# Two load queues instead of one: x from Sync, y from Scalar, in a kernel that streams 512 MB

## The chip, the cores and the metric

The kernel runs on one core of a Trainium2 chip (the experiments ran on two chips, each round with the kernel before beside it). The metric is the device time in microseconds (us), the median of several executions. All executions quoted here are of the undisturbed state ("fast"); those of one kernel agreed within 0.06% of each other. Engines: ACT is ScalarE, DVE is VectorE, POOL is GpSimd, PE is TensorE, SP is SyncE. "SPq" and "ACTq" are the sequencers of SP and ACT while they issue a DMA. Each engine takes its instructions in the order in which the build laid them out; how much that can cost is seen below, where ACT stands still for about 9 us in front of one small instruction. "Lnn" is line nn of the kernel's file. A load has "landed" when its completion is signalled to the engines that wait for it.

## The reference

```python
# x, y: 8192 x 8192 float32
x_norm = np.linalg.norm(x, axis=1, keepdims=True)
y_norm = np.linalg.norm(y, axis=1, keepdims=True)
return np.sum(x * y, axis=1) / (x_norm.squeeze() * y_norm.squeeze() + 1e-8)
```

One cosine similarity per row. Every input byte is read once: 2 x 256 MB. Per row there are three sums, xx, yy and xy, and at the end xy / sqrt(xx * yy).

## The kernel before

The rows are cut into 64 tiles of 128 rows. A tile is one load of x (128 x 8192 float32, 4 MB) and one of y. ACT squares and sums x and y, DVE multiplies x by y and sums. There are two buffers for x and two for y, so tile t+2 can be loaded when tile t is used up.

```python
    XCH = [(0, HALF), (HALF, n_cols)]                     # last x: two halves
    Q = n_cols // 8                                       # last y: 3 x 1 MB, 2 x 0.5 MB
    YCH = [(0, 2 * Q), (2 * Q, 4 * Q), (4 * Q, 6 * Q), (6 * Q, 7 * Q), (7 * Q, n_cols)]

    def issue_dma(t):
        if t == last:
            for a, b in XCH:
                nc.sync.dma_start(out=xtiles[t][:, a:b], in_=xv[t, :, a:b])
            for a, b in YCH:
                nc.sync.dma_start(out=ytiles[t][:, a:b], in_=yv[t, :, a:b])
        else:
            nc.sync.dma_start(out=xtiles[t], in_=xv[t])
            nc.sync.dma_start(out=ytiles[t], in_=yv[t])
    ...
    def compute_tile(t):            # DVE: sum(x*y); ACT: sum(x*x), then sum(y*y)
    ...
    def chain(cols, ps, sb, orows): # closes the tiles in cols
        nc.vector.tensor_tensor(out=nn[:, cols], in0=xx_acc[:, cols], in1=yy_acc[:, cols],
                                op=mybir.AluOpType.mult)
        nc.scalar.activation(out=den[:, cols], in_=nn[:, cols],
                             func=mybir.ActivationFunctionType.Sqrt)
        nc.vector.reciprocal(out=rcp[:, cols], in_=den[:, cols])
        ...                         # times xy on DVE, transpose on PE, copy, store
    for t in range(n_tiles - 1):
        if t + 2 < n_tiles:
            issue_dma(t + 2)
        compute_tile(t)
        if t == n_tiles - 3:        # early closing chain: tiles 0 to 61
            e = slice(0, last - 1)
            chain(e, res_t_ps[e, :], res_t[e, :], e)
    ...
    # last tile, in pieces. First: xx of columns 0:2048 on DVE, of 2048:4096 on ACT
    nc.scalar.activation(out=sq_s[:, HALF:], in_=xt[:, HALF:],        # second half of the last x
                         func=mybir.ActivationFunctionType.Square, accum_out=xxp[:, 2:3])
    for k, (a, b) in enumerate(YCH):
        nc.scalar.activation(out=sq_s[:, a:b], in_=yt[:, a:b], ...)       # yy of this piece
        nc.vector.tensor_tensor_reduce(... in0=xt[:, a:b], in1=yt[:, a:b] ...)  # xy of it
    ...                             # fold the pieces, close tiles 62 and 63, store
```

The early closing chain: one product `nn` on DVE, then one square root `den` on ACT, for the 62 tiles that are done. It is written after tile 61.

## Time and profile before

| | before |
|---|---|
| time, median | 1256.34 us |
| DMA engines busy | 99.5% |
| bytes per second over the span | 428 GB/s |
| ACT busy / DVE busy | 73% / 45% |
| period of a tile in the steady part | 19.4 us |

From the page of the kernel before: the span, the busy times, the bytes per second in 40 slices of the span, the one load queue, and the chain of waits that ended last.

```profile
span 1254.4 us, 933 instructions
...
PE 0.8 (0%) x2; PEld 0.2 (0%) x2; DVE 561.6 (45%) x147; ACT 915.0 (73%) x276; POOL 0.7 (0%) x6
...
GB/s 401 435 435 435 429 430 428 435 434 435 429 429 430 434 433 435 429 428 432 434 434 435 428 428 432 435 434 434 428 428 433 435 433 433 427 430 432 435 434 307
...
q1 hardware_dynamic: 19220, 536.91, 99.5%
...
DMA 76%; DVE 22%; SPq 1%; issue 1%; DVEq 0%; PE 0%; ACT 0%
```

The loads bind: the rate is level (427 to 435 GB/s) between the first slice and the last, and the chain is loads and the DVE product that frees the next buffer. Next, three groups of instructions of the same page (line, engine, operation, output and inputs, count; then busy us and mean ns of one; then idle us before them and what ended it).

```profile
L96 DVE CUSTOM_DVE_ANT_0 prod_s<-xt,yt 128x8192 bf16<-128x8192 f32 x63 | 547.6, 8692 | 687.5 <-DMA yt<-in_y_dram 687.5
L106 ACT ACTIVATE sq_s<-xt 128x8192 bf16<-128x8192 f32 x63 | 442.9, 7031 | 168.5 <-DMA xt<-in_x_dram 168.5
L112 ACT ACTIVATE sq_s<-yt 128x8192 bf16<-128x8192 f32 x63 | 443.0, 7031 | 164.2 <-DMA yt<-in_y_dram 164.2
```

ACT waits about 2.6 us twice a tile: x lands, is squared in 7.03 us, then y lands 9.7 us after x. What the end costs is read from the timeline of the kernel before (start us, length us, engine, line, operation; in brackets the idle time before it and what ended it):

```profile
1209.50 7.03 ACT L112 ACTIVATE sq_s<-yt 128x8192 bf16<-128x8192 f32 x1 [2.59 <-DMA yt<-in_y_dram]
1209.58 8.69 DVE L96 CUSTOM_DVE_ANT_0 prod_s<-xt,yt 128x8192 bf16<-128x8192 f32 x1 [10.72 <-DMA yt<-in_y_dram]
...
1218.20 0.22 DVE L120 TENSOR_TENSOR nn<-xx_acc,yy_acc 128x62 f32<-128x62 f32 x1
...
1218.45 0.26 ACT L124 ACTIVATE den<-nn 128x62 f32<-128x62 f32 x1 [1.83 <-DVE nn L120]
...
1219.22 7.03 ACT L106 ACTIVATE sq_s<-xt 128x8192 bf16<-128x8192 f32 x1 [0.51 <-DMA xt<-in_x_dram]
...
1228.94 7.03 ACT L112 ACTIVATE sq_s<-yt 128x8192 bf16<-128x8192 f32 x1 [2.60 <-DMA yt<-in_y_dram]
1228.99 8.69 DVE L96 CUSTOM_DVE_ANT_0 prod_s<-xt,yt 128x8192 bf16<-128x8192 f32 x1 [8.60 <-DMA yt<-in_y_dram]
...
1238.69 3.62 ACT L173 ACTIVATE sq_s<-xt 128x4096 bf16<-128x4096 f32 x1 [0.59 <-DMA xt<-in_x_dram]
...
1249.21 1.04 ACT L180 ACTIVATE sq_s<-yt 128x1024 bf16<-128x1024 f32 x1
```

The product and the square root of the early chain (L120, L124) run at 1218. When y of tile 62 lands at 1228.9, its x has long been squared. ACT's last square ends at 1250.25, about 2 us after the last bytes, and DVE's last product at 1250.77; the span ends 4.15 us after ACT's last square.

### The profile page before, as it was taken

What the parts mean: (1) busy time and instruction counts of PE and PEld (TensorE: products, weight loads), DVE (VectorE), ACT (ScalarE), POOL (GpSimd) and SP (SyncE); (2) the same over time, 40 slices, a digit from 0 to 9 for tenths busy, and PEclk for the clock granted to TensorE, in tenths of its full rate; (3) what the DMA queues carried; (4) which work ended last, traced back from release to release, by engine and by line L of the source; (5) the groups of instructions that cost most, each with busy time, mean ns of one, the idle gap of its engine ahead of it and who ended that gap; (6) DMA issues with size and microseconds to landing.
All of it is one profiled execution on the core that took longest, in us unless ns stands there. A gap on an engine that the chain in (4) does not pass through costs nothing.

```text
span 1254.4 us, 933 instructions
## 1 busy us (share of the span) xinstructions
PE 0.8 (0%) x2; PEld 0.2 (0%) x2; DVE 561.6 (45%) x147; ACT 915.0 (73%) x276; POOL 0.7 (0%) x6
## 2 busy tenths in 40 slices
PE   0000000000000000000000000000000000000000
PEld 0000000000000000000000000000000000000000
DVE  2354353443534535445354353453544525445356
ACT  5777767776777767776777767776777767776777
POOL 0000000000000000000000000000000000000000
DMA  9999999999999999999999999999999999999997
GB/s 401 435 435 435 429 430 428 435 434 435 429 429 430 434 433 435 429 428 432 434 434 435 428 428 432 435 434 434 428 428 433 435 433 433 427 430 432 435 434 307
DMA packets 19227, 536.97 MB, mean 428 GB/s; under 512 B 2132, under 2 KB 2196, under 8 KB 2452
## 3 DMA queue, kind: packets, MB, share of 16 engines
q1 hardware_dynamic: 19220, 536.91, 99.5%
q14 instruction: 7, 0.06, 0.0%
HBM read 536.87 MB, written 0.03 MB: 428 GB/s over the span
## 4 chain that ended last, share of the span: by engine, by line
DMA 76%; DVE 22%; SPq 1%; issue 1%; DVEq 0%; PE 0%; ACT 0%
DMA yt<-in_y_dram 76%; DVE prod_s L96 21%; SPq L63 1%; DVE prod_s L186 0%; DVEq L96 0%; SPq L64 0%; SPq L61 0%; SPq L59 0%; DVE xy_acc L96 0%; PE res_t_ps_last L221 0%; DVE res_row_last L222 0%; ACT den L212 0%; DVE rcp L216 0%; DVE res L217 0%; DVE xy_acc L204 0%
## 5 line engine op out<-in xcount | busy, mean ns | idle before, releaser
L96 DVE CUSTOM_DVE_ANT_0 prod_s<-xt,yt 128x8192 bf16<-128x8192 f32 x63 | 547.6, 8692 | 687.5 <-DMA yt<-in_y_dram 687.5
L106 ACT ACTIVATE sq_s<-xt 128x8192 bf16<-128x8192 f32 x63 | 442.9, 7031 | 168.5 <-DMA xt<-in_x_dram 168.5
L112 ACT ACTIVATE sq_s<-yt 128x8192 bf16<-128x8192 f32 x63 | 443.0, 7031 | 164.2 <-DMA yt<-in_y_dram 164.2
L112 ACT ACTIVATION_READ_ACCUMULATOR sq_s<-yt 128x1 f32 x63 | 11.8, 188 | 0.0
L106 ACT ACTIVATION_READ_ACCUMULATOR sq_s<-xt 128x1 f32 x63 | 11.8, 187 | 0.0
L186 DVE CUSTOM_DVE_ANT_0 prod_s<-xt,yt 128x2048 bf16<-128x2048 f32 (+1 forms) x5 | 9.2, 1864 | 1.6 <-DMA yt<-in_y_dram 1.5
L180 ACT ACTIVATE sq_s<-yt 128x2048 bf16<-128x2048 f32 (+1 forms) x5 | 7.8, 1551 | 0.0
L96 DVE DVE_READ_ACCUMULATOR2_ANT xy_acc<- 128x1 f32 x63 | 5.2, 83 | 0.0
L173 ACT ACTIVATE sq_s<-xt 128x4096 bf16<-128x4096 f32 x1 | 3.6, 3617 | 0.6 <-DMA xt<-in_x_dram 0.6
L157 DVE CUSTOM_DVE_ANT_0 prod_s<-xt 128x2048 bf16<-128x2048 f32 x1 | 2.3, 2291 | 0.0
L167 ACT ACTIVATE sq_s<-xt 128x2048 bf16<-128x2048 f32 x1 | 1.9, 1911 | 0.0
L70 ACT ACT_TABLE_LOAD x1 | 1.3, 1283 | 0.7 <-PEq L238 0.7
L124 ACT ACTIVATE den<-nn 128x62 f32<-128x62 f32 x1 | 0.3, 257 | 1.8 <-DVE nn L120 1.8
L71 ACT ACT_TABLE_LOAD x1 | 1.3, 1283 | 0.0
L133 PE MATMUL res_t_ps<-ident,res 128*62 128x128 f32 x1 | 0.4, 392 | 1219.7 <-DVE res L129 1219.7
L180 ACT ACTIVATION_READ_ACCUMULATOR sq_s<-yt 128x1 f32 x5 | 0.9, 186 | 0.0
L128 DVE RECIPROCAL rcp<-den 128x62 f32<-128x62 f32 x1 | 0.5, 541 | 0.3 <-ACT den L124 0.3
L134 DVE COPY res_t<-res_t_ps 62x128 f32<-62x128 f32 x1 | 0.3, 282 | 0.6 <-PE res_t_ps L133 0.6
L212 ACT ACTIVATE den<-nn 128x2 f32<-128x2 f32 x1 | 0.2, 204 | 0.4 <-DVE nn L208 0.4
L222 DVE COPY res_row_last<-res_t_ps_last 2x128 f32<-2x128 f32 x1 | 0.3, 278 | 0.5 <-PE res_t_ps_last L221 0.5
L186 DVE DVE_READ_ACCUMULATOR2_ANT xyp<- 128x1 f32 x5 | 0.4, 83 | 0.0
L221 PE MATMUL res_t_ps_last<-ident,res 128*2 128x128 f32 x1 | 0.4, 371 | 31.6 <-DVE res L217 31.6
(23 smaller groups left out, 3.8 us busy)
## 6 DMA issues: line engine op xcount, KB each, us to landing
xt<-in_x_dram SPq DMA_DIRECT2D x63, 4096.0 KB, 20.2
yt<-in_y_dram SPq DMA_DIRECT2D x63, 4096.0 KB, 29.5
xt<-in_x_dram SPq DMA_DIRECT2D x2, 2048.0 KB, 19.9
yt<-in_y_dram SPq DMA_DIRECT2D x3, 1024.0 KB, 24.0
yt<-in_y_dram SPq DMA_DIRECT2D x2, 512.0 KB, 27.1
out_dram<-res_t SPq DMA_DIRECT2D x1, 31.0 KB
out_dram<-res_row_last SPq DMA_DIRECT2D x1, 1.0 KB
```

The costliest lines, as they stand in the source:

```text
L63: nc.sync.dma_start(out=xtiles[t], in_=xv[t])
L70: nc.scalar.memzero(dummy)
L71: nc.scalar.sqrt(out=dummy, in_=dummy)
L96: nc.vector.tensor_tensor_reduce(out=prod_s, in0=xt, in1=yt, scale=1.0, scalar=0.0, op0=mybir.AluOpType.mult, op1=mybir.AluOpType.add, acc ...
L106: nc.scalar.activation(out=sq_s, in_=xt, func=mybir.ActivationFunctionType.Square, accum_out=xx_acc[:, t:t + 1],)
L112: nc.scalar.activation(out=sq_s, in_=yt, func=mybir.ActivationFunctionType.Square, accum_out=yy_acc[:, t:t + 1],)
L128: nc.vector.reciprocal(out=rcp[:, cols], in_=den[:, cols])
L157: nc.vector.tensor_tensor_reduce(out=prod_s[:, 0:SPL], in0=xt[:, 0:SPL], in1=xt[:, 0:SPL], scale=1.0, scalar=0.0, op0=mybir.AluOpType.mult ...
L167: nc.scalar.activation(out=sq_s[:, SPL:HALF], in_=xt[:, SPL:HALF], func=mybir.ActivationFunctionType.Square, accum_out=xxp[:, 1:2],)
L173: nc.scalar.activation(out=sq_s[:, HALF:], in_=xt[:, HALF:], func=mybir.ActivationFunctionType.Square, accum_out=xxp[:, 2:3],)
L180: nc.scalar.activation(out=sq_s[:, a:b], in_=yt[:, a:b], func=mybir.ActivationFunctionType.Square, accum_out=yyp[:, k:k + 1],)
L186: nc.vector.tensor_tensor_reduce(out=prod_s[:, a:b], in0=xt[:, a:b], in1=yt[:, a:b], scale=1.0, scalar=0.0, op0=mybir.AluOpType.mult, op1= ...
```

## The change

The intent is to have both streams in flight together, each from its own queue. So that ACT does not stand at an issue whose buffer is still in use while it has a tile to compute, the issue is moved behind the computation of the tile.

```diff
             for a, b in YCH:
-                nc.sync.dma_start(out=ytiles[t][:, a:b], in_=yv[t, :, a:b])
+                nc.scalar.dma_start(out=ytiles[t][:, a:b], in_=yv[t, :, a:b])
         else:
             nc.sync.dma_start(out=xtiles[t], in_=xv[t])
-            nc.sync.dma_start(out=ytiles[t], in_=yv[t])
+            nc.scalar.dma_start(out=ytiles[t], in_=yv[t])
...
     for t in range(n_tiles - 1):
+        compute_tile(t)
         if t + 2 < n_tiles:
             issue_dma(t + 2)
-        compute_tile(t)
```

## The prediction

> **What bounds it now.** The load stream. The page shows the 16 DMA engines 99.5% taken by one queue, 428 GB/s over the span and 428 to 435 in nearly every slice; ACT is busy 73%, DVE 45%. The chain of waits is 76% "DMA yt" and 21.5% the DVE product, whose end frees the next buffers. In the timeline each tile (two loads of 4 MB) takes 19.43 us: x lands, y 9.7 us later. ACT squares each in 7.03 us (+0.19 to read the sum) and then idles 2.6 us; DVE takes 8.69 us after y. The reload of a tile is issued 8.9 us after its y lands, with over 10 us of loads still queued, so the queue never runs dry. Nothing but bytes per second and the two ends can change the time.
>
> **What the change does.**
> 1. Issue: 68 y loads move from SP to ACT, at about 0.4 us each (SPq durations of 0.38 to 0.51). ACT's work per tile goes from 14.4 to about 15 us of 19.4. Off the path.
> 2. Streams: x(t) and y(t) share the engines and land together, every 19.43 us instead of 9.7 us apart. The Trainium skill ("DMA: Bandwidth & Descriptors", section "Issuing engines are not separate DMA queues") says that loads from several engines interleave on the same 16 DMA engines and only save issue time; its section "Queues, rings and completion order" says each engine alternates between queues packet by packet. The page's packet counts fit rows of 32 KB, so equal shares and no small-packet cost. I expect the bandwidth unchanged.
> 3. Refill: with both landing at T, DVE is done at T+8.8 (x reissued), ACT has squared both at T+14.5 (y reissued at about T+15). The next pair lands at T+19.4, so the y queue keeps about 4.5 us of work (an estimate from these durations). Neither queue empties; the moved issue costs nothing.
> 4. The end: here the change costs. Before, x of the last tile is in and squared while its y arrives; after the last bytes (about 1248.3 us, where the DMA share falls to zero in the windows) only 2 us of squaring is left, ACT working without gaps. After, the last two full tiles land together at about 1228.9, so ACT squares both until 1243.4, then the second quarter of the last x until 1245.3; the second half of that x lands only with the last y at about 1248.3, and ACT's program order has it ahead of all five y pieces: 3.6 + 3x1.89 + 2x1.04 = 11.4 us, to about 1259.8 instead of 1250.25. The closing chain of 4.15 us follows unchanged. That is +9.6 us, all on the path. DVE's three pieces after the wait take under 5 us and finish earlier.
> 5. The start: both first loads issue at about 0.7 us rather than 0.46 apart; the queue fills at most 0.5 us earlier.
>
> Sum: 1256.4 + 9.6 - 0.5 = 1265.5 us.
>
> **What the profile should show.** Two hardware queues with half the bytes each, together 99% busy, about 430 GB/s; y landing within 1 us of x; ACT waiting for DMA once a tile, some 4 to 5 us, instead of twice 2.6; SP's issue waits halved; the chain ending in ACT's squares of the last y, some 11 us after the last bytes, with a last slice of low GB/s.
>
> **What would make it wrong.** Alternating queues could hide the small gap between loads (19.43 us against 19.28 at the skill's ceiling of 435 GB/s: at most about 10 us in all), which would cancel the tail; or two streams could disturb the memory and cost per cent; or unequal shares let x run ahead, keeping the old order and the old tail (then 1256).

## The result, and the profile after

| | before | after |
|---|---|---|
| time, median | 1256.34 us | 1271.84 us |
| span of the profiled run | 1254.4 us | 1269.8 us |
| load rate between 100 and 1200 us | 432 GB/s | 432 GB/s |
| ACT starts squaring x of tile 62 | 1219.2 us | 1238.2 us |
| ACT's last square ends | 1250.25 us | 1265.7 us |

The ratio is 1.0123 (95% interval 1.0109 to 1.0138). Here and below a ratio is the mean time of one kernel's fast runs over that of the other's fast runs of the same rounds, so it is not quite the ratio of the medians quoted. The loss is 15.5 us; predicted were 9.1.

The page of the changed kernel:

```profile
span 1269.8 us, 874 instructions
...
PE 0.8 (0%) x2; PEld 0.2 (0%) x2; DVE 561.2 (44%) x147; ACT 914.4 (72%) x276; POOL 0.7 (0%) x6
...
GB/s 412 430 429 429 429 433 434 437 430 430 429 429 433 434 433 434 430 429 429 434 434 431 434 431 429 429 435 433 431 431 433 429 431 435 430 433 431 433 424 110
...
q10 hardware_dynamic: 9792, 268.44, 49.2%
q1 hardware_dynamic: 9428, 268.47, 49.2%
...
DMA 68%; issue 15%; DVE 11%; ACT 5%; DVEq 0%; PE 0%; SPq 0%
```

Two queues carry half the bytes each and together keep the DMA engines as busy as one did (98.4% of the longer span against 99.5%, and alike between 100 and 1200 us). The busy times of DVE and ACT are unchanged. Only the last slice differs much: 110 GB/s instead of 307. So the loss is at the end. The same stretch of the steady part, from the table of busy times by stretch (the last two columns are the DMA share and GB/s), first before:

```profile
100.00:1200.00 1100.00, 0.00 (x0) 0.00 (x0) 495.91 (x114) 805.19 (x227) 0.00 (x0) 1.00 1.00 432
```

and after:

```profile
100.00:1200.00 1100.00, 0.00 (x0) 0.00 (x0) 495.91 (x114) 807.77 (x227) 0.00 (x0) 1.00 1.00 432
```

The groups after show the intended overlap: ACT now waits once a tile, 334.0 us over 62 waits (the first took 19.6 us, the others 5.2 us each), and never for y, which has landed by the time x is squared.

```profile
L96 DVE CUSTOM_DVE_ANT_0 prod_s<-xt,yt 128x8192 bf16<-128x8192 f32 x63 | 547.6, 8693 | 689.7 <-DMA yt<-in_y_dram 656.2
L106 ACT ACTIVATE sq_s<-xt 128x8192 bf16<-128x8192 f32 x63 | 442.9, 7030 | 334.0 <-DMA xt<-in_x_dram 334.0
L112 ACT ACTIVATE sq_s<-yt 128x8192 bf16<-128x8192 f32 x63 | 442.9, 7030 | 1.9
```

The timeline of the end of the changed kernel, where the 15 us are:

```profile
1223.68 5.46 ACTq L61 DMA_DIRECT2D yt<-in_y_dram  x5
1229.13 8.69 DVE L96 CUSTOM_DVE_ANT_0 prod_s<-xt,yt 128x8192 bf16<-128x8192 f32 x1 [10.66 <-DMA yt<-in_y_dram]
...
1237.74 0.22 DVE L120 TENSOR_TENSOR nn<-xx_acc,yy_acc 128x62 f32<-128x62 f32 x1
...
1238.00 0.26 ACT L124 ACTIVATE den<-nn 128x62 f32<-128x62 f32 x1 [14.35 <-DVE nn L120]
1238.16 7.01 ACT L106 ACTIVATE sq_s<-xt 128x8192 bf16<-128x8192 f32 x1
...
1245.30 7.03 ACT L112 ACTIVATE sq_s<-yt 128x8192 bf16<-128x8192 f32 x1
...
1254.36 3.60 ACT L173 ACTIVATE sq_s<-xt 128x4096 bf16<-128x4096 f32 x1
...
1264.67 1.04 ACT L180 ACTIVATE sq_s<-yt 128x1024 bf16<-128x1024 f32 x1
```

Tile 62 is there at about 1229, for DVE uses it from 1229.13. ACT does not. It stands at the square root L124 of the early chain, which waits for L120; and L120, which ran at 1218 before, is now laid out on DVE behind the 8.69 us product of tile 62. The two instructions close tiles 0 to 61, whose sums have been complete since 1223.6. The build's order for the two engines (not a profile; instructions as laid out, bare waits left out; tile 62's product is the one that reads `xt_138`), lines of difference of the changed kernel on DVE against the kernel before:

```
 L96 ISA prod_s,xy_acc<-xt_137,yt_201 128x8192
 L96 ISA xy_acc 128x1
-L120 TensorTensor nn<-xx_acc,yy_acc 128x62
-L128 Reciprocal rcp<-den 128x62
-L129 TensorTensor res<-xy_acc,rcp 128x62
-L134 TensorCopy res_t<-res_t_ps 62x128
 L96 ISA prod_s,xy_acc<-xt_138,yt_202 128x8192
 L96 ISA xy_acc 128x1
+L120 TensorTensor nn<-xx_acc,yy_acc 128x62
...
```

On ACT the square root is still laid out ahead of the squares of tile 62, as it was before. ACT did not step past it: of the 14.35 us without work, the first 5.46 went to the y issues, and for the other 8.9 it stood there with tile 62 in its buffers.

So there are four suspects for the 15.5 us. Theory A: this square root, and besides it the two tiles near the end that land with x and y together. Rival B: the y issues on ACT; the first line of the timeline has five of them taking 5.46 us, the last of which starts only at 1228.8, as it shares a completion count with the load of x of tile 62 and waits for that load to land. Rival C: the loads of the two queues are slower somewhere. Rival D: the new loop order does it by itself.

### The profile page after: what moved, and what is told of

It reads as the page before. It is cut to its first block, busy times and chain, and to the rows that moved or that the text cites. A ratio compares the mean times of both kernels' runs of the same rounds, so it can differ in the third digit from the quotient of the medians.

```text
span 1269.8 us, 874 instructions
## 1 busy us (share of the span) xinstructions
PE 0.8 (0%) x2; PEld 0.2 (0%) x2; DVE 561.2 (44%) x147; ACT 914.4 (72%) x276; POOL 0.7 (0%) x6
## 2 busy tenths in 40 slices
DMA packets 19227, 536.97 MB, mean 423 GB/s; under 512 B 2132, under 2 KB 2196, under 8 KB 2452
## 4 chain that ended last, share of the span: by engine, by line
DMA 68%; issue 15%; DVE 11%; ACT 5%; DVEq 0%; PE 0%; SPq 0%
DMA xt<-in_x_dram 36%; DMA yt<-in_y_dram 32%; DVE prod_s L96 11%; ACT sq_s L112 3%; ACT sq_s L106 2%; ACT sq_s L180 1%; ACT L71 0%; DVEq L96 0%; PE res_t_ps_last L221 0%; DVE xy_acc L96 0%; SPq L63 0%; DVE res_row_last L222 0%; ACT sq_s L173 0%; ACT sq_s L167 0%; ACT den L212 0%
## 5 line engine op out<-in xcount | busy, mean ns | idle before, releaser
L106 ACT ACTIVATE sq_s<-xt 128x8192 bf16<-128x8192 f32 x63 | 442.9, 7030 | 334.0 <-DMA xt<-in_x_dram 334.0
L112 ACT ACTIVATE sq_s<-yt 128x8192 bf16<-128x8192 f32 x63 | 442.9, 7030 | 1.9
L112 ACT ACTIVATION_READ_ACCUMULATOR sq_s<-yt 128x1 f32 x63 | 11.7, 186 | 0.0
L124 ACT ACTIVATE den<-nn 128x62 f32<-128x62 f32 x1 | 0.3, 255 | 14.3 <-DVE nn L120 14.3
## 6 DMA issues: line engine op xcount, KB each, us to landing
xt<-in_x_dram SPq DMA_DIRECT2D x2, 2048.0 KB, 25.4
```

The source lines that it names most:

```text
L106: nc.scalar.activation(out=sq_s, in_=xt, func=mybir.ActivationFunctionType.Square, accum_out=xx_acc[:, t:t + 1],)
L112: nc.scalar.activation(out=sq_s, in_=yt, func=mybir.ActivationFunctionType.Square, accum_out=yy_acc[:, t:t + 1],)
```

## The experiments

Eleven kernels ran. Each gave correct results. All ratios are against the kernel before in the same rounds.

### 1. The loop order alone

```diff
-                nc.scalar.dma_start(out=ytiles[t][:, a:b], in_=yv[t, :, a:b])
+                nc.sync.dma_start(out=ytiles[t][:, a:b], in_=yv[t, :, a:b])
...
-            nc.scalar.dma_start(out=ytiles[t], in_=yv[t])
+            nc.sync.dma_start(out=ytiles[t], in_=yv[t])
```

(Against the changed kernel: only compute-then-issue is left of the change.)

> Only the loop order of the change (compute, then issue), all loads still on Sync. The instructions laid out on ACT, DVE and SP come out as before. Theory A (the square root of the first 62 tiles waits on ACT behind DVE's product of tile 62, 6 us, and the rest is two tiles landing together): 1256.4 us. Rival B (the issues on ACT hold it at the end): 1256.4. Rival D (the new loop order itself costs the extra 6 us): about 1262.

Measured: 1256.33 us, ratio 0.9999 (0.9984 to 1.0014). D falls. The build lays the closing chain out as in the kernel before, so the loop order alone does not displace L120. The other half, the y loads on ACT with the old loop order, was not run. It was built: every engine's instructions come out in the order of the changed kernel. So what displaced L120 is moving the y loads to ACT, not the loop.

### 2. The product ahead of the square root moved off DVE

```diff
     def chain(cols, ps, sb, orows):
-        nc.vector.tensor_tensor(
+        nc.gpsimd.tensor_tensor(
             out=nn[:, cols], in0=xx_acc[:, cols], in1=yy_acc[:, cols],
```

> The change, with the one product xx*yy of the first 62 tiles moved from DVE to GpSimd, so that ACT's square root behind it need not wait for DVE's product of tile 62; all else on ACT stays in place, the five y issues too. A: ACT starts squaring x of tile 62 at about 1229.2 instead of 1238.2, then waits 3 us for the last half of x at 1248.4, and ends the squares at 1259.9: 1266.1 us. B (the y issues): no change, 1271.8. C (slower loads): no change, 1271.8.

Measured: 1263.0 us, ratio 1.0052 (1.0036 to 1.0069), 8.8 us less than the change. A's cause is right, B and C fall: the five issues are still on ACT, and the load rate was not touched. The size was off, though, 1263.0 instead of 1266.1. The timeline of this run, ACT at the end:

```profile
1229.17 0.26 ACT L124 ACTIVATE den<-nn 128x62 f32<-128x62 f32 x1 [5.53 <-DMA xt<-in_x_dram]
1229.48 7.03 ACT L106 ACTIVATE sq_s<-xt 128x8192 bf16<-128x8192 f32 x1
...
1245.70 3.60 ACT L173 ACTIVATE sq_s<-xt 128x4096 bf16<-128x4096 f32 x1
...
1256.02 1.04 ACT L180 ACTIVATE sq_s<-yt 128x1024 bf16<-128x1024 f32 x1
```

ACT starts on tile 62 8.7 us earlier (1229.48 instead of 1238.16), and all of it shows in the time. The 3 us of waiting for the second half of the last x that the prediction had did not happen: at 1245.70 that half was there. Experiment 6 asks why.

### 3. Only the last tile's y back on Sync

```diff
             for a, b in YCH:
-                nc.scalar.dma_start(out=ytiles[t][:, a:b], in_=yv[t, :, a:b])
+                nc.sync.dma_start(out=ytiles[t][:, a:b], in_=yv[t, :, a:b])
```

> The change, with only the last tile's five y pieces back on Sync, behind its x. The square root is now laid out after the square of x of tile 62. A: ACT squares x62 from 1229.2, waits for DVE only from 1236.3 to 1238.0, has the last x early and needs no wait for it, ends the squares at about 1258.7: 1265 us. B: only the 3.3 us between the fourth and the fifth issue come off: 1268.5. C: 1271.8.

Measured: 1264.58 us, ratio 1.0064 (1.0049 to 1.0079), near A's 1265. B alone (1268.5) is too little. Here the build laid the square root between the squares of x and of y of tile 62. ACT squared x at once and then waited 2.01 us for L120:

```profile
1228.96 7.03 ACT L106 ACTIVATE sq_s<-xt 128x8192 bf16<-128x8192 f32 x1 [5.23 <-DMA xt<-in_x_dram]
...
1238.09 0.26 ACT L124 ACTIVATE den<-nn 128x62 f32<-128x62 f32 x1 [2.01 <-DVE nn L120]
```

### 4. No early closing chain

```diff
-        if t == n_tiles - 3:
-            e = slice(0, last - 1)
-            chain(e, res_t_ps[e, :], res_t[e, :], e)
...
-    tcols = slice(last - 1, last + 1)
+    tcols = slice(0, last + 1)
```

(The closing transpose, copy and store are widened from 2 to 64 rows in the same way.)

> The change without the early closing chain: all 64 tiles closed at the end, so there is no square root before the last tiles at all. A: as with the product on GpSimd, plus some 0.5 us for the wider closing chain (reciprocal 0.54 instead of 0.17 us): 1266.6. B and C: 1272.3.

Measured: 1264.08 us, ratio 1.0061 (1.0046 to 1.0076). With no square root in the way at all, the time is again some 8 us below the change, so the result of experiment 2 does not hang on GpSimd. It missed the expected 1266.6 by about what experiment 2 missed its own. The time is 1.1 us over experiment 2, not 0.5: from ACT's last square to the end it takes 5.5 us instead of 4.0, and ACT is done 0.3 us earlier.

### 5. The control: the same move in the kernel before

The one-line edit of experiment 2, applied to the kernel before.

> Control: the kernel before with the same product moved from DVE to GpSimd. There the square root never waited for the product of tile 62, so nothing can be gained: 1256.4 us. If the move helped by itself, about 1248 (8.8 less, as in the changed kernel).

Measured: 1256.38 us, ratio 0.9999 (0.9986 to 1.0013). Here the square root waits as long as it did on DVE (1.83 us there), in time in which the x of tile 62 has not landed:

```profile
1218.47 0.26 ACT L124 ACTIVATE den<-nn 128x62 f32<-128x62 f32 x1 [1.86 <-POOL nn L120]
```

The move by itself is worth nothing. So the 8.8 us are a cost that the change brought.

### 6. Why the last x came early

A look at the loads of the changed kernel between 1228.9 and 1238.0 us, when only the last tile is under way (queue, packets, MB, share of the DMA engines; q1 is SP's queue with x, q10 is ACT's with y):

```profile
q1 hardware_dynamic: 173, 2.57, 67.3%
q10 hardware_dynamic: 174, 1.29, 34.0%
```

A packet is the unit in which the page counts what the DMA engines moved. As many packets on each queue, but twice the bytes for x. The last x is loaded in halves, with 16 KB in each row; the last y in pieces with 8 and 4 KB in each row. The Trainium skill, "DMA: Bandwidth & Descriptors", section "Queues, rings and completion order", says that an engine round-robins between the queues at packet granularity. If a packet is a row, a queue with longer rows gets more bytes. The test gives the last y the same rows as x, leaving the computation as it is, on top of experiment 2 (the build lays three small instructions of the early closing chain earlier on DVE, which is off the path: at the end DVE waits 6.5 us for ACT):

```diff
-            for a, b in YCH:
+            for a, b in XCH:
                 nc.scalar.dma_start(out=ytiles[t][:, a:b], in_=yv[t, :, a:b])
```

> The change with the product on GpSimd, and the last y loaded in two halves of 16 KB rows as x is, instead of five pieces of 8 and 4 KB rows. Theory S (queues share by packets, so 16 KB rows of x against 8 KB rows of y gave x two thirds, and the last x was in 4 us early): now both last halves land at about 1248.3, ACT waits for the second half of x from 1245.6 to 1248.3: about 1265.8 us against 1263.0 with five pieces. Rival (x was early for another reason, as the late issue of y): no wait, 1263.

Measured: 1266.59 us, ratio 1.008 (1.0066 to 1.0094), 3.6 us more than with five pieces. In the same stretch the queues now share equally:

```profile
q10 hardware_dynamic: 133, 1.95, 50.3%
q1 hardware_dynamic: 131, 1.92, 50.3%
```

and ACT waits for the second half of x as the prediction had it:

```profile
1248.59 3.62 ACT L173 ACTIVATE sq_s<-xt 128x4096 bf16<-128x4096 f32 x1 [4.38 <-DMA xt<-in_x_dram]
```

Theory S holds, and the rival falls: the y loads were issued about as late here, from 1222.8 against 1223.7. In the changed kernel the second half of the last x, issued at 1218.9, landed 25.4 us later, at about 1244.3; here it landed at about 1248.6. The loads of the last x in the changed kernel (view of the tile xt):

```profile
L59 SPq DMA_DIRECT2D xt<-in_x_dram x2: 328/376/425, 1218.5 to 1218.9; - x2
...
DMA to landing us min/median/max: 25.4/25.4/25.4
```

The wait is longer than the 2.7 us expected because in this run x of tile 62 landed about 1 us sooner, so that ACT began tile 62 at 1227.90 and was done with it sooner; the end of the wait, not its start, sets the time.

### 7. What the remaining 6.6 us are

After the square root is out of the way, 1263.0 - 1256.4 = 6.6 us are left. Two tiles land with x and y together near the end: 62 and 63. First, only tile 62 is left to do so: experiment 2 with the edit of experiment 3 on top.

> The change with the product on GpSimd and the last y back on Sync behind its x: nothing of the last tile lands together any more, only tile 62 does. Theory A (what is left, 6.6 us, is ACT's backlog of two squares when tile 62 lands at 1229; ACT then works without a gap whatever the order of the last tile): 1263.0 us, no gain. Rival (what is left comes from the last tile's x and y landing together): about 1256.5 to 1258.

Measured: 1262.52 us, ratio 1.0049 (1.0033 to 1.0064). The order of the last tile is worth 0.5 us at most, and hardly that: over the kernel before of the same rounds this run is 6.25 us longer (1256.27 there), experiment 2 was 6.36 (1256.64). The rest is tile 62. Its x and y land together, so ACT has one more 7.03 us square to do at 1229 than before, and from there it works without a gap to the end:

```profile
1228.91 7.03 ACT L106 ACTIVATE sq_s<-xt 128x8192 bf16<-128x8192 f32 x1 [5.23 <-DMA xt<-in_x_dram]
...
1236.09 7.01 ACT L112 ACTIVATE sq_s<-yt 128x8192 bf16<-128x8192 f32 x1
...
1255.45 1.04 ACT L180 ACTIVATE sq_s<-yt 128x1024 bf16<-128x1024 f32 x1
```

Then the last two, and the last three tiles all from Sync, again on top of experiment 2:

```diff
-            nc.scalar.dma_start(out=ytiles[t], in_=yv[t])
+            q = nc.sync if t == last - 1 else nc.scalar     # three tiles: t >= last - 2
+            q.dma_start(out=ytiles[t], in_=yv[t])
```

(and the last y on Sync as in experiment 3)

> Two streams up to tile 61, then the last two tiles all on Sync, x before y as before; the product of the first 62 tiles on GpSimd. Theory A (what is left after the square root is that tiles near the end land with x and y together, so that ACT has two squares to do at once; the two streams cost nothing in the middle): ACT still has 14.3 us to do when tile 61 lands at 1209.4, catches up 5 us in tile 62, and is about 1.3 us late at the end: 1257.6 us. Theory C (two streams make the loads slower all along, or a fixed cost of the second queue): about 1263, as with both tiles on two queues.

> The same with the last three tiles on Sync: ACT has one tile more to catch up in. A: no lag left at the end, 1256.4 us, the time of the kernel before, although 61 of 64 tiles come over two queues. C: about 1263.

Measured: 1257.43 us, ratio 1.0008 (0.9993 to 1.0024), and 1256.91 us, ratio 1.0004 (0.999 to 1.0017). A's numbers hold within about 0.5 us, C is far off. With three tiles on Sync, ACT has caught up: it waits for y of tile 62 again, as in the kernel before (an added line makes L112 into L113 here):

```profile
1229.09 7.03 ACT L113 ACTIVATE sq_s<-yt 128x8192 bf16<-128x8192 f32 x1 [2.57 <-DMA yt<-in_y_dram]
```

With 61 of 64 tiles on two queues, the time is within 0.5 us of the kernel before (1256.39 us in those rounds): in the middle the two streams cost nothing that can be told here, and gain nothing.

### 8. Two tries for a better kernel

Both start from the kernel before, on one queue. The first loads and uses y of tile 62 in halves, so that the engines begin the work of the end earlier:

```diff
+        elif t == last - 1:
+            nc.sync.dma_start(out=xtiles[t], in_=xv[t])
+            for a, b in XCH:
+                nc.sync.dma_start(out=ytiles[t][:, a:b], in_=yv[t, :, a:b])
```

(with the squares and the product of that tile in the same halves, added on GpSimd)

> Not a test of the change but a try for a better kernel: the kernel before (one queue), with y of tile 62 loaded and used in two halves, so that both engines start 2.6 us (ACT) and more (DVE) earlier on the work of the end, which the kernel before does without a gap from 1236 to 1250. Expected: the end bound by the last bytes at 1248.3 instead: 1255.3 us, 0.1% faster than before.

The second also gives DVE a quarter of the last x to square and cuts the third 1 MB piece of the last y in two:

```diff
+    nc.vector.tensor_tensor_reduce(out=prod_s[:, HALF:HALF + SPL],
+        in0=xt[:, HALF:HALF + SPL], in1=xt[:, HALF:HALF + SPL], ...)
```

> Second try for a better kernel, on one queue: y of tile 62 in halves, y of the last tile in pieces of 1, 1 and four of 0.5 MB, and a quarter of the last x squared on DVE, which sat idle for 5 us there in the first try. Expected: the last piece lands at 1248.4, and both engines are done 1.2 us later, at about 1249.7 instead of 1250.8: 1255.3 us.

Measured: 1256.37 us, ratio 1.0 (0.9988 to 1.0013), and 1256.39 us, ratio 1.0 (0.9988 to 1.0013). Neither gains. In the second one, DVE starts on the last y when its first piece lands, at 1241.47, and then multiplies its six pieces in 9.3 us almost without a gap, to 1250.7, as before. The work on the last y, not the work carried over from tile 62, sets the end there. The expectation had overlooked that DVE needs nearly as long for the last y as its loading takes.

## Why the prediction was right or wrong

The direction, the place and the kind of loss were right; the time was 6.3 us too low, 1265.5 against 1271.84 us, a loss of 9.1 us where 15.5 were measured. Point by point:

1. Loads bind, and two queues do not change their rate: right. 432 GB/s before and after between 100 and 1200 us. What the Trainium skill says in "DMA: Bandwidth & Descriptors", section "Issuing engines are not separate DMA queues", agrees with this trace.
2. The small gap between loads could be hidden by a second queue: it was not; the rate stayed at 432.
3. The start gains up to 0.5 us: wrong. ACT issued the first y at 0.73 us instead of 1.20, but DVE began its first product at 22.82 us after the change and at 22.77 before.
4. The refill has slack: right. In the steady part the queues did not run dry, though y lags x by a little more than the 1 us predicted in some tiles (DVE, which needs both, starts at 62.65 where ACT starts on x at 61.38). That SP's waits would be halved was wrong: 1174.0 us instead of 1144.1 in the waits of its queue, since before, too, it waited only once a tile.
5. The end, predicted as +9.6 us, is the step that failed, and in two of its terms.
   - "The last two full tiles land together at about 1228.9, so ACT squares both until 1243.4". Only one full tile lands there, 62; tile 61 had landed at 1209.4. The slip is in the words: the sum used the two squares of tile 62. What failed is the start. ACT began at 1238.16, because the build had laid the square root of the early closing chain in front of them and the product that feeds it behind DVE's 8.69 us product of tile 62. The prediction took the order of instructions from the program's text and from the kernel before, and did not ask whether moving 68 loads to ACT would lay the others out anew. Taking this wait away gave 8.8 us (experiment 2).
   - "The second half of that x lands only with the last y at about 1248.3". It was there by about 1244.3, since in the last tile the shares were two thirds and one third, not equal. "The page's packet counts fit rows of 32 KB, so equal shares" is true of all tiles but the last. With the square root out of the way this is worth 3.6 us: with equal rows 1266.59 us, with unequal ones 1263.0 (experiment 6). In the changed kernel itself it is worth nothing, as ACT, late as it is, comes to that half only at 1254.36.
   - What remains of the predicted mechanism, the joint landing near the end, measured 6.6 us (experiments 2 and 7).
6. Together: ACT began tile 62 9.3 us later than predicted. About 3 us of this were absorbed, since an engine so late no longer waits for the last x; its squares ended at 1265.7 instead of 1259.8, 5.9 us late. With the 0.5 us that the start did not gain, that is the miss of 6.3 us to 0.1. That the wrong shares do not show in the time is luck: ACT was late for another reason. With both failed terms put right, in experiment 6 (no wait for the product, equal rows), the time was 1266.59 us, 1.1 from the predicted 1265.5: the rest of the sum was sound. The split of the loss into 6.6 us (tiles landing together) and 8.8 us (square root) adds up by construction, both being differences to experiment 2, and it holds for these row lengths: with equal rows the square root would be worth about 5.2 us (an estimate, 1271.84 - 1266.59; this was not run).

Rival B was not nothing: the fifth issue did hold ACT until 1229.1. But the x it would have worked on landed only at about 1228.8, and in the first run of experiment 7, without these issues, ACT began at 1228.91 instead of 1229.48: worth 0.6 us at most.

What stays open: why the build put the product behind tile 62 once the y loads were on ACT. The runs show that it did, that the loop order is not the reason, and what it cost; they do not show how the order is chosen.

## What to carry to other kernels

The loads already kept the DMA engines full here, and a second queue gave no more bytes per second. It changed when things land: two inputs that came one after the other came together, and near the end, where nothing later could absorb it, the engine that handles both had the work of the first one left over. And after any edit that moves instructions between engines, compare the order of instructions on every engine before reading it from the program: here a small closing step laid in front of a large one cost 8.8 us, more than the 6.6 us of the edit's own effect.

## What the Trainium skill lacked or had wrong

- "DMA: Bandwidth & Descriptors", section "Queues, rings and completion order": it says that queues alternate by packet, and that a packet is typically 9 to 17 descriptors. It does not say what follows for two streams with different row lengths. Here 16 KB rows against 8 KB rows gave 173 and 174 packets but 2.57 and 1.29 MB, and equal rows gave 1.92 and 1.95 MB. The packet counts of the profile, if they count the same packets, fit one row for each packet, not 9 to 17: of 19227 packets 16775 are of 8 KB or more, and the tiles have 16768 such rows.
- The same page, section "Issuing engines are not separate DMA queues": it says that several issuers save only issue time. The rate agrees (432 GB/s both ways). It does not mention that loads issued from ACT stand in ACT's own order of instructions, where a load that must wait holds the computation behind it: five y issues took 5.46 us there. Other passages have the premises, that an engine's queue is in order and that a load's wait sits on the issuing sequencer; this consequence was found in none.
- The same page, section "Where 436 GB/s comes from": it says that for loads from HBM a limit of about 358 GB/s binds, and in the next sentence calls a measured 425 near the fabric's rate. With a program on one core, this case measured 432 GB/s in the steady part, so the limit did not bind here. The page "HBM Reference", section "Specifications (TRN2)", is nearer with about 425 for a core streaming alone.
